# Gates with both activation halves as one 512-column matmul, and decay matrices loaded as broadcast rows through GpSimd's queue

## The chip, the cores and the metric

The kernel runs on one core of one Trainium2 chip. The metric is the device time of one execution in microseconds (us); the median of the runs stands for the kernel. The engines are named as in the profile: PE is TensorE's matmul side and PEld its weight loads, DVE is VectorE, ACT is ScalarE, POOL is GpSimd, SP is SyncE. A line such as L366 is a line of the kernel's file.

## The reference

Two layers of a hybrid model run over 256 tokens of width 2048 (batch 1), in float32. The first ("even") layer has a bidirectional gated delta rule, a differential attention and an attention over 256 memory tokens; the second ("odd") layer has a window attention, a latent attention and a memory attention. Each layer projects the normed input to all queries, keys, values and gates, multiplies every branch's output by a gated silu, and projects back.

```
h = rms_norm(x, norm_g) @ w_in
gq, gk, gv, gb, ga, gg, dq, dk, dv, dg, mq, mg = split_cols(h, EV_SPLITS)
y = concat([gdn_branch(...), diff_attention(...), memory_attention(...)])
return x + y @ w_out
```

The part that matters here is the decay of the delta rule, and the gate:

```
g = jnp.cumsum(g, axis=-1)                       # per chunk of 64, per head and direction
diff = g[..., :, None] - g[..., None, :]
decay = jnp.where(lower_incl, jnp.exp(jnp.where(lower_incl, diff, 0.0)), 0.0)
m = jnp.where(strict, jnp.einsum('bhncd,bhnsd->bhncs', k_beta, k) * decay, 0.0)
a_intra = jnp.where(lower_incl, jnp.einsum('bhncd,bhnsd->bhncs', q, k) * decay, 0.0)
o = o * jax.nn.silu(gate)                        # each branch
```

## The kernel before

**Matmuls in halves.** Every float32 weight and activation is split into a high half that the PE takes (fp32r) and a low rest. A product is then three matmuls: weights high by activations high, weights high by activations low, weights low by activations high. `load_split` brings a block of weights `w` (128 rows by 1024 columns, 512 KB) over SP's queue (L194), casts it to `wh` on ACT (L201) and subtracts `wl = w - wh` on DVE (L202). The activations lie channel-major in two tiles, `xH` and `xL` (16 tiles of 128 channels by 256 tokens).

**Three kinds of projection.** `gemm` (L218 to L220) has tokens on the output's partitions and streams up to 512 weight columns. `gemm_T` (L233 to L235) and `gate_T` (L365 to L367) are channel-major: 128 weight columns stay in the PE and the 256 tokens of `xH` or `xL` stream through. `gate_T` makes 256 gate channels from 16 channel tiles, two accumulators and three matmuls each, in twelve calls: 2 in the even layer (L965's loop), 10 in the odd one. Its two accumulators are scaled by `rsb` on DVE (L370), then come tanh on ACT (L371) and two multiplications on DVE (L372, L373). `gemm_out` (L254 to L256) is the output projection; it goes through the channel blocks of `y` in an order written out, for the even layer 8, 12, 16, 0, 4. Blocks 0 and 4 are the delta rule's output `o_gdn`, transposed on the PE by `gated_T` (L392) and split into halves by ACT (L154) and DVE (L155).

**The delta rule** works on two groups of four heads, two 128-token tiles `t` and two directions `d`. `gdn_rates` makes the cumulated decay `gcum` early (by 124 us). `keys_decay` makes for each group the keys `kT` (with `qk_tiles`, whose convolution on DVE and ACT writes the tiles `cc`, L697 to L704), and then for each `t` and `d` the decay matrix `E` (128 by 4x128): four PE transposes of a broadcast column of `gcum` (L757), four DVE instructions that subtract the column and add the mask (L759), and one exponential on ACT (L761). Later lines build `MnT` from it, invert triangles by substitution on DVE, and run the chunks: matmuls into `z` (L892) and `o` (L922), then add (L924), a sum of squares on ACT, a power on POOL (L145), scaling into `o_gdn` (L932) and the last gate multiplication (L352).

**What sets the order.** The Tile framework's scheduler orders each engine's instructions by its own simulated timeline, within the dependences of the tiles; `tc.issue_after(x)` holds an instruction until `x`. Each engine works through its row in order, and each DMA queue through its own. So a change in one place can move instructions far from it.

Of the kernel before, what the change touches and what calls it, by code (L numbers as in the profile page):

```python
# [87 lines left out]
def kernel(ctx: ExitStack, tc: tile.TileContext, a: dict, out: bass.AP):  # L88
# [46 lines left out]
    def bcm(ap, n):  # L135

        return ap.unsqueeze(1).to_broadcast([ap.shape[0], n, ap.shape[1]])

    def inv_sqrt(out_ap, ss, mul, eps, st="n"):

        shape = [ss.shape[0], ss.free_size()]
        t = spool.tile([P, 32], F32, tag="isq" + st, name="isq")
        tv = t[:shape[0], :shape[1]]
        V.tensor_scalar(tv, ss, mul, eps, op0=ALU.mult, op1=ALU.add)  # L144
        G.tensor_tensor(out_ap, tv, mhalf[:shape[0], :shape[1]], op=ALU.pow)  # L145

# [207 lines left out]

    def gate_T(wd, col, oT, H, L, rsb, pool, y=None):


        wv = wd.rearrange("(k p) c -> p k c", p=P)
        acc = [accp.tile([P, 512], F32, tag="acc", name="acc")[:, :S] for _ in range(2)]
        for k0 in range(0, NK, 4):  # L360
            wh, wl = load_split(wv[:, k0:k0 + 4, col:col + 256], 4, 256)
            for k in range(4):
                for i in range(2):
                    cs, kk = slice(i * P, (i + 1) * P), k0 + k
                    T.matmul(acc[i], lhsT=wh[:, k, cs], rhs=H[:, kk], start=kk == 0, stop=False)  # L365
                    T.matmul(acc[i], lhsT=wh[:, k, cs], rhs=L[:, kk], start=False, stop=False)  # L366
                    T.matmul(acc[i], lhsT=wl[:, k, cs], rhs=H[:, kk], start=False, stop=kk == NK - 1)  # L367
        g_, th = [pool.tile([P, 512], F32, tag="gt", name=n, bufs=4).rearrange("p (i s) -> p i s", i=2) for n in ("g_", "gth")]
        for i in range(2):
            V.tensor_tensor(g_[:, i], acc[i], rsb, op=ALU.mult)  # L370
        A.activation(th, g_, AF.Tanh, scale=0.5)  # L371
        V.scalar_tensor_tensor(th, th, 1.0, g_, op0=ALU.add, op1=ALU.mult)  # L372
        V.tensor_tensor(th if y else oT, th, oT, op=ALU.mult)  # L373
        if y:
            split(th, None, *y)
# [32 lines left out]

    xH = xpool.tile([P, NK, S], F32R, tag="xH", name="xH")
    xL = xpool.tile([P, NK, S], F32R, tag="xL", name="xL")  # L410

    bias_d = dpool.tile([2, 8, 512], F32, name="bias_d")
    NG = 480
    sg_d = dpool.tile([P, 2, NG], F32, name="sg_d")
# [106 lines left out]
    with tc.tile_pool(name="dif", bufs=2, reuse_waits="tile") as dp:  # L521
# [85 lines left out]
        def gdn_rates():  # L607
# [52 lines left out]
            V.tensor_tensor(be2, beta, e2, op=ALU.mult)  # L660
            return rsb, beta, nbeta, gl, gcum, e1, ne1, e2, be2

        qkv = diff_qkv(0)
        mem_split(0)
        rsb, beta, nbeta, gl, gcum, e1, ne1, e2, be2 = gdn_rates()
        diff_attention(0, *qkv)
# [57 lines left out]
    def cols_of(h0):  # L724
# [3 lines left out]
        return cols  # L728

    def keys_decay(h0):  # L730

        cols = cols_of(h0)


        kN = gp.tile([P, 2, 4, P], F32, tag="kN", name="kN", bufs=2)
        kT, ssk = qk_tiles(EV["gk"] + h0 * P, 8 + h0, "k", kN)
        rk, r2k, irk = [keep(8) for _ in range(3)]
        nb2, b2, be22 = [keep(16).rearrange("p (t d h) -> p t d h", t=2, d=2) for _ in range(3)]
        inv_sqrt(rk, ssk, 1.0, 4 * EPS)
        V.tensor_tensor(r2k, rk, rk, op=ALU.mult)  # L740
        V.scalar_tensor_tensor(irk, ssk, 4 * EPS, rk, op0=ALU.add, op1=ALU.mult)
        V.tensor_scalar(irk, irk, 0.5, None, op0=ALU.mult)
        r2b = r2k.rearrange("p (t h) -> p t h", t=2).unsqueeze(2).to_broadcast([P, 2, 2, 4])
        for dst, src in ((nb2, nbeta), (b2, beta), (be22, be2)):
            V.tensor_tensor(dst, src.rearrange("p (t d h) -> p t d h", t=2, d=2)[:, :, :, h0:h0 + 4], r2b, op=ALU.mult)

        E = gp.tile([P, 2, 2, 4, P], F32, tag="E", name="E", bufs=2)
        MnT = gp.tile([P, 2, 2, 4, P], F32, tag="MnT", name="MnT", bufs=2)
        for t in range(2):
            pg = ps_tile()  # L750
            for h in range(4):
                T.matmul(pg[:, h * P:(h + 1) * P], lhsT=kT[:, h, t * P:(t + 1) * P], rhs=kT[:, h, t * P:(t + 1) * P],
                         start=True, stop=True)
            for d in range(2):
                pb = ps_tile()
                for h in range(4):
                    T.transpose(pb[:, h * P:(h + 1) * P], cols(gcum, t, d)[:, h:h + 1].to_broadcast([P, P]), ident)  # L757
                for h in range(4):
                    V.scalar_tensor_tensor(E[:, d, t, h], pb[:, h * P:(h + 1) * P], cols(gcum, t, d)[:, h:h + 1],  # L759
                                           amask(d), op0=ALU.subtract, op1=ALU.add)  # L760
                A.activation(E[:, d, t], E[:, d, t], AF.Exp)  # L761
                for h in range(4):
                    V.scalar_tensor_tensor(MnT[:, d, t, h], pg[:, h * P:(h + 1) * P], nb2[:, t, d, h:h + 1],
                                           E[:, d, t, h], op0=ALU.mult, op1=ALU.mult)
        m_d = dpool.tile([16, 4, 32, 32], F32, tag="m_d", name="m_d", bufs=2)
        mv_ = MnT.rearrange("p d t h c -> p (d t h) c")
        for b in range(4):
            nc.sync.dma_start(m_d[:, b].rearrange("m i j -> i m j"), mv_[b * 32:(b + 1) * 32, :, b * 32:(b + 1) * 32])
        return kN, kT, E, MnT, irk, b2, be22, m_d.rearrange("m b i j -> (m b) i j")

# [13 lines left out]
    G.memset(vt, 0.0)  # L784
    G.memset(vt.rearrange("p i j -> p (i j)")[:, 0:1024:33], 1.0)
    tmp = gp.tile([P, 256], F32, name="tmp")
# [19 lines left out]
    for grp in range(2):  # L806
# [4 lines left out]
        Tm = gp.tile([P, 2, 2, 4, P], F32, tag="Tm", name="Tm")  # L811
        G.memset(Tm, 0.0)
        for dst, src in zip((Tm, Rm), tr_d[grp]):
# [129 lines left out]
    for g in range(2):  # L943
        hs = slice(2 * g, 2 * g + 2)
        gate_T(w0, EV["mg"] + 256 * g, o_mem[:, hs], xH, xL, rsb, opool2)
    for t in range(2):
# [9 lines left out]
    with tc.tile_pool(name="yp", bufs=2, reuse_waits="tile") as yp:  # L956
# [7 lines left out]
        def evac(g, t, ps):  # L964
            if not nxt:  # L965
                nxt.extend(xpool.tile([P, NK, S], F32R, tag=n, name=n + "1") for n in ("xH", "xL"))
            x_ = x1[:, t, 512 * g:512 * (g + 1)]
# [5 lines left out]
            if t == 1:  # L973
                split_T(lambda k, t: x1[:, t, k * P:(k + 1) * P], par[:, R_ODN:R_ODN + NK], range(4 * g, 4 * g + 4), *nxt)
        gemm_out(a["ev_w_out"][0], y, (8, 12, 16, 0, 4), evac,
                 [(4 * i, lambda i=i: gated_T(cols512(o_gdn, i), par[:, R_GDN:R_GDN + 1], y[4 * i])) for i in range(2)])
        opool_stack.close()
        xH, xL = nxt
        ss1 = spool.tile([P, 2], F32, tag="ssx", name="ss1")
# [13 lines left out]
    def gates(col, o_, k0, n):  # L993
        for g in range(0, n, 2):
            gate_T(w1, col + P * g, o_[:, g:g + 2], xH, xL, rsb1, yp, [x_[:, g % 4:g % 4 + 2] for x_ in y[k0 + g - g % 4]])

# [205 lines left out]
```

## Time and profile before

| what | value |
|---|---|
| median of 3 runs | 1206.33 us (1205.81 to 1206.83) |
| the profiled execution | 1208.67 us, span in the trace 1206.9 us |
| PE busy | 1190.3 us, 99% of the span |
| DVE, ACT, POOL busy | 839.8 (70%), 640.0 (53%), 109.8 us (9%) |
| granted clock of PE | 0.996 of full speed over the span |

The span is what the trace covers, from the first instruction to the last; the execution's own time is 1.8 us longer. The sums of the prediction are made on the profiled execution and then moved to the median, which lies 2.34 us lower. A busy PE is not a PE at its peak: a matmul counts as busy from its start to its modelled end, and consecutive ones overlap, so the distance from start to start says more than the mean of one.

### The profile page before, as it was taken

Reading aid. Unit: us, or ns where it says so; the run is one execution under the profiler, and the core shown is the slowest. Engines: PE = TensorE matmul, PEld = TensorE weight load, DVE = VectorE, ACT = ScalarE, POOL = GpSimd, SP = SyncE. Lnnn points to the kernel's source line nnn. Section 1 sums busy time; section 2 is a strip of 40 time slices with the busy share of each in tenths; the row PEclk is TensorE's granted clock in tenths of the full one; section 3 lists DMA queues with packets and bytes.
Section 4 is the critical chain, followed back from the end, with each engine's and each line's share of the span. In section 5 each row is a group of like instructions: output and inputs, shape, how many; then the busy total and the mean of one; then the engine's idle time right before and its main releaser. Section 6 shows DMA issues by size and latency. Waiting matters only on the chain.

```text
span 1206.9 us, 19842 instructions
## 1 busy us (share of the span) xinstructions
PE 1190.3 (99%) x7608; PEld 1063.2 (88%) x7608; DVE 839.8 (70%) x1450; ACT 640.0 (53%) x1117; POOL 109.8 (9%) x116
## 2 busy tenths in 40 slices
PE   9899999999999999999999999999999999999998
PEld 7678888788999999889988889999889899998887
DVE  5675876666889899857755555667766678876553
ACT  6664666455555454444654446566555555554432
POOL 0110112000101010002000001323310000000000
PEclk9899999999999999999999999999999999999999
DMA  9976675555655666653536656666556565555663
GB/s 333 350 225 230 215 236 162 175 165 167 174 152 137 168 176 192 194 142 82 187 105 209 206 167 185 179 184 194 160 158 203 164 208 158 159 157 166 201 210 121
DMA packets 183183, 221.95 MB, mean 184 GB/s; under 512 B 20536, under 2 KB 119608, under 8 KB 182576
## 3 DMA queue, kind: packets, MB, share of 16 engines
q1 hardware_dynamic: 172640, 201.09, 56.0%
q10 hardware_dynamic: 9552, 16.48, 3.9%
q0 software_dynamic: 896, 3.11, 0.8%
q8 instruction: 59, 0.97, 0.3%
q14 instruction: 36, 0.29, 0.1%
HBM read 214.36 MB, written 6.29 MB: 183 GB/s over the span
## 4 chain that ended last, share of the span: by engine, by line
PE 89%; DVE 4%; DMA 3%; ACT 2%; issue 1%; POOL 1%; SPq 0%; DVEq 0%; ACTq 0%; POOLq 0%
PE acc L219 14%; PE acc L220 13%; PE acc L218 13%; PE acc L254 6%; PE acc L256 6%; PE acc L255 6%; PE acc L366 4%; PE acc L367 4%; PE acc L365 4%; PE acc L235 3%; PE acc L233 3%; PE acc L234 3%; PE ps L165 3%; PE ps L892 1%; DVE wl L202 1%
## 5 line engine op out<-in xcount | busy, mean ns | idle before, releaser
L202 DVE TENSOR_TENSOR wl<-w,wh 128x1024 fp32r<-128x1024 f32 (+3 forms) x392 | 456.8, 1167 | 240.5 <-ACT wh L201 237.9
L201 ACT CAST wh<-w 128x1024 fp32r<-128x1024 f32 (+3 forms) x392 | 392.1, 1001 | 401.4 <-PE acc L220 141.3
L219 PE MATMUL acc<-wl,xH 128*128 128x512 f32 (+3 forms) x704 | 259.5, 370 | 3.0 <-DVE wl L202 3.0
L220 PE MATMUL acc<-wh,xL 128*128 128x512 f32 (+3 forms) x704 | 256.0, 365 | 0.0
L218 PE MATMUL acc<-wh,xH 128*128 128x512 f32 (+3 forms) x704 | 238.5, 366 | 2.7 <-ACT wh L201 2.7
L219 PEld LDWEIGHTS acc<-wl,xH 128*128 128x128 f32 x704 | 133.1, 189 | 24.2 <-DVE wl L202 5.4
L218 PEld LDWEIGHTS acc<-wh,xH 128*128 128x128 f32 x704 | 130.5, 189 | 21.1 <-ACT wh L201 4.2
L220 PEld LDWEIGHTS acc<-wh,xL 128*128 128x128 f32 x704 | 133.1, 189 | 17.1
L255 PE MATMUL acc<-wl,y 128*128 128x512 f32 x320 | 124.9, 391 | 0.0
L256 PE MATMUL acc<-wh,y 128*128 128x512 f32 x320 | 124.4, 390 | 0.0
L254 PE MATMUL acc<-wh,y 128*128 128x512 f32 x320 | 115.3, 392 | 1.3 <-ACT y L154 1.3
L235 PE MATMUL acc<-xH,wl 128*128 128x256 f32 x384 | 109.4, 286 | 1.1 <-DVE wl L202 1.1
L365 PE MATMUL acc<-xH,wh 128*128 128x256 f32 x384 | 110.1, 287 | 0.0
L366 PE MATMUL acc<-xL,wh 128*128 128x256 f32 x384 | 109.9, 286 | 0.0
L367 PE MATMUL acc<-xH,wl 128*128 128x256 f32 x384 | 109.6, 286 | 0.0
L233 PE MATMUL acc<-xH,wh 128*128 128x256 f32 x384 | 109.3, 285 | 0.0
L234 PE MATMUL acc<-xL,wh 128*128 128x256 f32 x384 | 109.1, 284 | 0.0
L145 POOL TENSOR_TENSOR r<-isq,kept 128x4 f32<-128x4 f32 (+2 forms) x27 | 49.7, 1841 | 400.4 <-DVE isq L144 384.1
L235 PEld LDWEIGHTS acc<-xH,wl 128*128 128x128 f32 x384 | 73.4, 191 | 1.7 <-DVE wl L202 1.7
L366 PEld LDWEIGHTS acc<-xL,wh 128*128 128x128 f32 x384 | 74.2, 193 | 0.3
L365 PEld LDWEIGHTS acc<-xH,wh 128*128 128x128 f32 x384 | 74.3, 194 | 0.2
L367 PEld LDWEIGHTS acc<-xH,wl 128*128 128x128 f32 x384 | 74.1, 193 | 0.0
(364 smaller groups left out, 1760.9 us busy)
## 6 DMA issues: line engine op xcount, KB each, us to landing
w<-in_ev_w_in_dram SPq DMA_DIRECT2D x136, 512.0 KB, 4.1
w<-in_od_w_in_dram SPq DMA_DIRECT2D x72, 512.0 KB, 3.9
w<-in_ev_w_out_dram SPq DMA_DIRECT2D x40, 512.0 KB, 3.7
w<-in_od_w_out_dram SPq DMA_DIRECT2D x40, 512.0 KB, 4.1
w<-in_od_w_in_dram SPq DMA_DIRECT2D x32, 384.0 KB, 3.4
w<-in_od_mem_w_kv_dram SPq DMA_DIRECT2D x16, 512.0 KB, 3.6
w<-in_ev_mem_w_kv_dram SPq DMA_DIRECT2D x16, 512.0 KB, 3.7
w<-in_od_w_in_dram SPq DMA_DIRECT2D x16, 288.0 KB, 2.9
```

The costliest lines, as they stand in the source:

```text
L201: A.copy(wh[:, :kn * n], w[:, :kn * n])
L202: V.tensor_tensor(wl[:, :kn * n], w[:, :kn * n], wh[:, :kn * n].bitcast(F32), op=ALU.subtract)
L218: T.matmul(o, lhsT=h, rhs=wh[:, k], start=first, stop=False)
L219: T.matmul(o, lhsT=h, rhs=wl[:, k], start=False, stop=False)
L220: T.matmul(o, lhsT=l, rhs=wh[:, k], start=False, stop=last)
L235: T.matmul(o, lhsT=wl[:, k], rhs=H[:, kk], start=False, stop=kk == NK - 1)
L254: T.matmul(acc[t], lhsT=h, rhs=wh[:, k], start=first, stop=False)
L255: T.matmul(acc[t], lhsT=h, rhs=wl[:, k], start=False, stop=False)
L256: T.matmul(acc[t], lhsT=l, rhs=wh[:, k], start=False, stop=last)
L365: T.matmul(acc[i], lhsT=wh[:, k, cs], rhs=H[:, kk], start=kk == 0, stop=False)
L366: T.matmul(acc[i], lhsT=wh[:, k, cs], rhs=L[:, kk], start=False, stop=False)
L367: T.matmul(acc[i], lhsT=wl[:, k, cs], rhs=H[:, kk], start=False, stop=kk == NK - 1)
```

## The change

`xH` and `xL` become the two halves of one tile `xHL` (channel tile, half, token), so that a channel tile's two halves lie side by side as 512 columns. `gate_T` streams them through the high weights in one matmul of 512 columns into a whole accumulator (now L369), and the low weights by the high activations into its first 256 columns (L370). Behind it ACT copies the second half out, DVE adds it to the first, and one DVE multiplication scales both channels.

For the decay matrices, `gdn_rates` transposes `gcum` once, writes the 32 rows to a scratch tensor in DRAM (`gc_d`), and makes `ngcum`, the negated column. `keys_decay` loads each `E[:, d, t]` (128 by 512, 256 KB) from four rows of `gc_d`, broadcast to all partitions: 8 DMAs on GpSimd's queue, held behind `held`, the last power (`inv_sqrt`) written before `keys_decay`. DVE then adds the mask in one instruction of 512 columns, and ACT takes four exponentials of 128 columns, each with its column of `ngcum` as bias. The PE transposes and the 32 DVE instructions go. A clearing of `Tm` on POOL is held behind that of the substitution's identity.

```diff
     def inv_sqrt(out_ap, ss, mul, eps, st="n"):
...
-        G.tensor_tensor(out_ap, tv, mhalf[:shape[0], :shape[1]], op=ALU.pow)
+        pows.append(G.tensor_tensor(out_ap, tv, mhalf[:shape[0], :shape[1]], op=ALU.pow))
+        return pows[-1]
...
-    def gate_T(wd, col, oT, H, L, rsb, pool, y=None):
+    def gate_T(wd, col, oT, HL, rsb, pool, y=None):
...
-        acc = [accp.tile([P, 512], F32, tag="acc", name="acc")[:, :S] for _ in range(2)]
+        acc = [accp.tile([P, 512], F32, tag="acc", name="acc") for _ in range(2)]
...
-                    T.matmul(acc[i], lhsT=wh[:, k, cs], rhs=H[:, kk], start=kk == 0, stop=False)
-                    T.matmul(acc[i], lhsT=wh[:, k, cs], rhs=L[:, kk], start=False, stop=False)
-                    T.matmul(acc[i], lhsT=wl[:, k, cs], rhs=H[:, kk], start=False, stop=kk == NK - 1)
+                    T.matmul(acc[i], lhsT=wh[:, k, cs], rhs=HL[:, kk].rearrange("p h s -> p (h s)"), start=kk == 0, stop=False)
+                    T.matmul(acc[i][:, :S], lhsT=wl[:, k, cs], rhs=HL[:, kk, 0], start=False, stop=kk == NK - 1)
...
-            V.tensor_tensor(g_[:, i], acc[i], rsb, op=ALU.mult)
+            A.copy(g_[:, i], acc[i][:, S:])
+            V.tensor_tensor(g_[:, i], acc[i][:, :S], g_[:, i], op=ALU.add)
+        V.tensor_tensor(g_, g_, bcm(rsb, 2), op=ALU.mult)
...
+            ngcum = sm("ngcum")
+            V.tensor_scalar(ngcum, gcum, -1.0, None, op0=ALU.mult)
+            pt = ps_tile()
+            T.transpose(pt[:32, :P], gcum, ident)
+            gr = dp.tile([32, P], F32, name="gr", bufs=1)
+            V.tensor_copy(gr, pt[:32, :P])
+            G.dma_start(gc_d, gr)
...
+    held = pows[-1].ins
...
+        E = gp.tile([P, 2, 2, 4, P], F32, tag="E", name="E", bufs=2)
+        for t in range(2):
+            for d in range(2):
+                r_ = gc_d[t * 16 + d * 8 + h0:t * 16 + d * 8 + h0 + 4]
+                with tc.issue_after(held):
+                    G.dma_start(E[:, d, t].rearrange("p h c -> p (h c)"), bass.AP(r_.tensor, r_.offset, [[0, P], [1, 4 * P]]))
...
-                pb = ps_tile()
+                V.tensor_tensor(E[:, d, t], E[:, d, t], bcm(amask(d), 4), op=ALU.add)
                 for h in range(4):
-                    T.transpose(pb[:, h * P:(h + 1) * P], cols(gcum, t, d)[:, h:h + 1].to_broadcast([P, P]), ident)
-                for h in range(4):
-                    V.scalar_tensor_tensor(E[:, d, t, h], pb[:, h * P:(h + 1) * P], cols(gcum, t, d)[:, h:h + 1],
-                                           amask(d), op0=ALU.subtract, op1=ALU.add)
-                A.activation(E[:, d, t], E[:, d, t], AF.Exp)
+                    A.activation(E[:, d, t, h], E[:, d, t, h], AF.Exp, bias=cols(ngcum, t, d)[:, h:h + 1])
...
-    G.memset(vt.rearrange("p i j -> p (i j)")[:, 0:1024:33], 1.0)
+    eye = G.memset(vt.rearrange("p i j -> p (i j)")[:, 0:1024:33], 1.0)
...
-        G.memset(Tm, 0.0)
+        with tc.issue_after(eye.ins):
+            G.memset(Tm, 0.0)
```

The scheduler then orders the rows anew. On GpSimd's row the eight loads of `E` stand in one block directly behind the held power `r<-isq` (128 by 8), and ahead of the powers of the keys (`kept<-isq`). The changed kernel's row there:

```order
L147 TENSOR_TENSOR r<-isq,kept 128x4 x2
L147 TENSOR_TENSOR r<-isq,kept 128x8
L761 DMA E<-gc_d 128x512 x8
L147 TENSOR_TENSOR kept<-isq,kept 128x8 x2
L805 MEMSET Rm 128x1024
```

In the kernel before, the same power was followed by the keys' powers at once:

```order
L145 TENSOR_TENSOR r<-isq,kept 128x4 x2
L145 TENSOR_TENSOR r<-isq,kept 128x8
L145 TENSOR_TENSOR kept<-isq,kept 128x8 x2
L784 MEMSET Rm 128x1024
```

On DVE's row the eight additions of the mask (L780), for both groups, stand among the convolution of the next keys and the subtractions `wl` (now L205), a little behind the scaling of the memory queries (`nat`). The changed kernel's row from that scaling on:

```order
L280 TENSOR_TENSOR nat<-acc,r 128x512 x2
L715 TENSOR_TENSOR kept<-acc,kept 128x256
L205 TENSOR_TENSOR wl<-w,wh 128x1024
L780 TENSOR_TENSOR E<-E,kept 128x512
L719 SCALAR_TENSOR_TENSOR cc<-kept,cc 128x256
L780 TENSOR_TENSOR E<-E,kept 128x512
...
L780 TENSOR_TENSOR E<-E,kept 128x512 x2
L293 TENSOR_REDUCE nm<-ps 128x2
L780 TENSOR_TENSOR E<-E,kept 128x512 x2
L205 TENSOR_TENSOR wl<-w,wh 128x1024
L722 SCALAR_TENSOR_TENSOR kT<-kT,cc 128x256
```

Between the two `wl` shown stand a third one and all eight additions. Before, the same place held no work for `E`; the 32 DVE instructions of L759 stood after the keys' convolution, and the `kT` of the last row stood ahead of the last `wl` shown.

On PE's row the end of the delta rule (group 1's last matmuls `ps<-Tm,E`, before L922, now L944) moves behind nearly the whole output projection of the blocks 8, 12 and 16. Before:

```order
L922 MATMUL ps<-Tm,E 128x128
L255 MATMUL acc<-wl,y_6514 128x512
...
L254 MATMUL acc<-wh,y_6514 128x512
L922 MATMUL ps<-Tm,E 128x128 x15
L255 MATMUL acc<-wl,y_6514 128x512
...
L254 MATMUL acc<-wh,y_6515 128x512 x2
L392 MATMUL acc<-kept,o_gdn 128x128 x4
L255 MATMUL acc<-wl,y_6515 128x512
```

Here 28 matmuls of the projection stand between the last L922 and the first transposes of `o_gdn` (L392). In the changed kernel:

```order
L259 MATMUL acc<-wh,y_6431 128x512
L397 MATMUL acc<-kept,o_gdn 128x128 x2
L944 MATMUL ps<-Tm,E 128x128
L397 MATMUL acc<-kept,o_gdn 128x128 x4
L944 MATMUL ps<-Tm,E 128x128 x15
L397 MATMUL acc<-kept,o_gdn 128x128
L257 MATMUL acc<-wh,y_6427 128x512
L258 MATMUL acc<-wl,y_6427 128x512
...
L259 MATMUL acc<-wh,y_6427 128x512
L397 MATMUL acc<-kept,o_gdn 128x128 x5
```

The lone transpose (L397) behind the fifteen L944 takes the columns 384 to 511 of `o_gdn`, of the first token tile. The last 32 of them are gated by the same multiplication (columns 480 to 751, now L355) that needs group 1's output; and the first matmul of block 0 behind it (L257) needs that transpose, split into halves. Only 12 matmuls of the projection then stand between it and the next transposes.

## Rows read from the trace of the kernel before

**Rows 1.** The page: busy time of each engine; GB/s in 40 slices.
```profile
PE 1190.3 (99%) x7608; PEld 1063.2 (88%) x7608; DVE 839.8 (70%) x1450; ACT 640.0 (53%) x1117; POOL 109.8 (9%) x116
...
GB/s 333 350 225 230 215 236 162 175 165 167 174 152 137 168 176 192 194 142 82 187 105 209 206 167 185 179 184 194 160 158 203 164 208 158 159 157 166 201 210 121
```

**Rows 2.** Waits of TensorE, whole span: us in total, times, longest.
```profile
PE acc L254 <- ACT y L154: 1.3, 1, 1.3
PE acc L235 <- DVE wl L202: 1.1, 2, 0.7
PE ps L892 <- ACT MnT L905: 1.0, 1, 1.0
```

**Rows 3.** Timeline of PE, a gate_T, then the output projection: start, us, line.
```profile
1089.38 0.28 PE L367 MATMUL acc<-xH,wl 128*128 128x256 f32 x1
...
1090.82 0.28 PE L367 MATMUL acc<-xH,wl 128*128 128x256 f32 x1
...
1093.26 0.40 PE L256 MATMUL acc<-wh,y 128*128 128x512 f32 x1
...
1094.42 0.39 PE L255 MATMUL acc<-wl,y 128*128 128x512 f32 x1
...
1100.09 0.39 PE L256 MATMUL acc<-wh,y 128*128 128x512 f32 x1
```

**Rows 4.** Groups by line, the decay matrices: busy us, mean ns.
```profile
L759 DVE SCALAR_TENSOR_TENSOR E<-ps,kept 128x128 f32<-128x128 f32 x32 | 9.0, 353 | 0.3 <-PE ps L757 0.3
```

**Rows 5.** Timeline of PE, the first four decay transposes and the row behind.
```profile
368.25 0.60 PE L757 MATMUL ps<-kept 128*128 128x128 f32 x4
368.60 0.36 PE L234 MATMUL acc<-xL,wh 128*128 128x256 f32 x1
```

**Rows 6.** Stretches: busy PE, PEld, DVE, ACT, POOL; clock, DMA share, GB/s.
```profile
320.00:330.00 10.00, 10.00 (x86) 10.00 (x85) 9.29 (x20) 6.08 (x11) 0.00 (x0) 1.00 0.60 164
...
368.00:395.00 27.00, 27.00 (x234) 27.00 (x233) 26.55 (x81) 14.80 (x23) 4.41 (x2) 1.00 0.51 132
```

**Rows 7.** Timeline of POOL, DVE and PE, 309 to 327 us.
```profile
309.21 2.62 POOL L145 TENSOR_TENSOR r<-isq,kept 128x8 f32<-128x8 f32 x1 [4.19 <-DVE isq L144]
...
313.11 1.28 DVE L277 TENSOR_TENSOR nat<-acc,r 128x512 f32<-128x512 f32 x2
...
314.31 0.42 DVE L697 TENSOR_TENSOR kept<-acc,kept 128x256 f32<-128x256 f32 x1
...
321.52 1.22 DVE L202 TENSOR_TENSOR wl<-w,wh 128x1024 fp32r<-128x1024 f32 x1
...
326.36 0.28 PE L235 MATMUL acc<-xH,wl 128*128 128x256 f32 x1
```

**Rows 8.** DMA issues of GpSimd's queue: KB each, median us to landing.
```profile
mk_d<-kT POOLq DMA_DIRECT2D x2, 512.0 KB, 4.8
mv_d<-mvN POOLq DMA_DIRECT2D x2, 512.0 KB, 3.8
...
sg<-sg_d POOLq DMA_DIRECT2D x2, 240.0 KB, 5.4
```

**Rows 9.** Timeline of POOL, the two issues of mv_d.
```profile
159.51 0.53 POOL L604 DMA_DIRECT2D mv_d<-mvN  x1 [9.60 <-ACT mvN L154]
160.37 0.53 POOL L604 DMA_DIRECT2D mv_d<-mvN  x1 [0.34 <-DVE mvN L155]
```

**Rows 10.** Timeline of DVE and PE, end of the delta-rule block, group 1.
```profile
612.96 0.69 DVE L924 TENSOR_TENSOR MnT<-ps,MnT 128x512 f32<-128x512 f32 x1 [3.90 <-PE ps L922]
...
616.22 1.23 DVE L202 TENSOR_TENSOR wl<-w,wh 128x1024 fp32r<-128x1024 f32 x1 [0.58 <-ACT wh L201]
...
618.34 0.80 DVE L352 TENSOR_TENSOR o_gdn<-th,o_gdn 128x272 f32<-128x272 f32 x2
...
623.62 0.60 PE L392 MATMUL acc<-kept,o_gdn 128*128 128x128 f32 x4
...
625.50 0.50 PE L254 MATMUL acc<-wh,y 128*128 128x512 f32 x1 [1.29 <-ACT y L154]
```

More of the change, by code (lines that the diff above doesn't have):

```diff
@@ L137, in bcm @@
         return ap.unsqueeze(1).to_broadcast([ap.shape[0], n, ap.shape[1]])
+    pows = []
     def inv_sqrt(out_ap, ss, mul, eps, st="n"):
@@ L407, with both_halves @@
     opool_stack = ExitStack()
-    xH = xpool.tile([P, NK, S], F32R, tag="xH", name="xH")
-    xL = xpool.tile([P, NK, S], F32R, tag="xL", name="xL")
+    def both_halves(name):
+        x_ = xpool.tile([P, NK, 2, S], F32R, tag="xHL", name=name)
+        return x_, x_[:, :, 0], x_[:, :, 1]
+    xHL, xH, xL = both_halves("xHL0")
     bias_d = dpool.tile([2, 8, 512], F32, name="bias_d")
+    gc_d = dpool.tile([32, P], F32, name="gc_d")
     NG = 480
@@ L660, in gdn_rates @@
             V.tensor_tensor(be2, beta, e2, op=ALU.mult)
-            return rsb, beta, nbeta, gl, gcum, e1, ne1, e2, be2
+            ngcum = sm("ngcum")
[5 more added lines that the diff above has]
+            G.dma_start(gc_d, gr)
+            return rsb, beta, nbeta, ngcum, e1, ne1, be2
         qkv = diff_qkv(0)
         mem_split(0)
-        rsb, beta, nbeta, gl, gcum, e1, ne1, e2, be2 = gdn_rates()
+        rsb, beta, nbeta, ngcum, e1, ne1, be2 = gdn_rates()
         diff_attention(0, *qkv)
@@ L745, in keys_decay @@
             V.tensor_tensor(dst, src.rearrange("p (t d h) -> p t d h", t=2, d=2)[:, :, :, h0:h0 + 4], r2b, op=ALU.mult)
-        E = gp.tile([P, 2, 2, 4, P], F32, tag="E", name="E", bufs=2)
         MnT = gp.tile([P, 2, 2, 4, P], F32, tag="MnT", name="MnT", bufs=2)
@@ L944 @@
         hs = slice(2 * g, 2 * g + 2)
-        gate_T(w0, EV["mg"] + 256 * g, o_mem[:, hs], xH, xL, rsb, opool2)
+        gate_T(w0, EV["mg"] + 256 * g, o_mem[:, hs], xHL, rsb, opool2)
     for t in range(2):
@@ L965, in evac @@
             if not nxt:
-                nxt.extend(xpool.tile([P, NK, S], F32R, tag=n, name=n + "1") for n in ("xH", "xL"))
+                nxt.extend(both_halves("xHL1"))
             x_ = x1[:, t, 512 * g:512 * (g + 1)]
@@ L973, in evac @@
             if t == 1:
-                split_T(lambda k, t: x1[:, t, k * P:(k + 1) * P], par[:, R_ODN:R_ODN + NK], range(4 * g, 4 * g + 4), *nxt)
+                split_T(lambda k, t: x1[:, t, k * P:(k + 1) * P], par[:, R_ODN:R_ODN + NK], range(4 * g, 4 * g + 4), *nxt[1:])
         gemm_out(a["ev_w_out"][0], y, (8, 12, 16, 0, 4), evac,
@@ L977 @@
         opool_stack.close()
-        xH, xL = nxt
+        xHL, xH, xL = nxt
         ss1 = spool.tile([P, 2], F32, tag="ssx", name="ss1")
@@ L994, in gates @@
         for g in range(0, n, 2):
-            gate_T(w1, col + P * g, o_[:, g:g + 2], xH, xL, rsb1, yp, [x_[:, g % 4:g % 4 + 2] for x_ in y[k0 + g - g % 4]])
+            gate_T(w1, col + P * g, o_[:, g:g + 2], xHL, rsb1, yp, [x_[:, g % 4:g % 4 + 2] for x_ in y[k0 + g - g % 4]])
     with tc.tile_pool(name="at1", bufs=2, reuse_waits="tile") as dp:
```

## The prediction

> **What bounds the kernel now.** I read the page first: PE is busy for 99% of the span, DVE for 70%, ACT for 53%, GpSimd for 9% [rows 1]. So time goes down in two ways only: fewer or shorter matmuls on PE, or fewer waits of PE. The waits come next: those that the change touches are 1.3 us for the halves of `y`, 1.1 us in two waits of `gemm_T` (L235) for `wl`, and 1.0 us inside the delta rule [rows 2]. Then I read the PE's timeline for what a matmul costs, which is the distance from one start to the next and not the mean in the groups: between 256-column matmuls it is 0.120 us (12 steps from 1089.38 to 1090.82), between 512-column ones 0.227 us (25 steps from 1094.42 to 1100.09), but 0.232 in the first five behind 256-column ones (1093.26 to 1094.42) [rows 3]. Last come the two places where instructions move: the stretch from 309 to 327 us [rows 7] and the end of the delta rule at 612 to 626 us [rows 10].
>
> **gate_T: -5.0 us.** 12 calls x 16 channel tiles x 2 accumulators are 384 groups. Three matmuls of 256 columns cost 0.36 us; one of 512 and one of 256 cost 0.347 us [rows 3]. The difference, 13 ns, times 384 is 5.0 us. It says that a matmul costs some 13 ns beyond what its columns cost, once each. Since the new matmuls change between 512 and 256 columns, the step of 0.232 could hold throughout; then it is 8 ns and 3.1 us, the other bound. I take 5.0, as the longer run shows the steady step. The evacuation grows by two ACT copies and a DVE addition per call, all behind the accumulators and ahead of a tanh whose reader comes later; DVE has 30% idle, so I cost it at nothing. If that cover were gone, each of the twelve calls could cost about one 512-column addition, 0.6 us [rows 7].
>
> [...]
>
> **Decay transposes: -2.7 us.** Four transposes (L757) hold PE for 0.35 us (368.25 to 368.60) [rows 5]; 32 of them, one for each instruction of L759 [rows 4], are eight such fours, 2.8 us. One new transpose of `gcum` gives back 0.1.
>
> **DVE after 368 us: -1.1 us.** DVE is busy 26.55 of 27 us at 368 to 395 [rows 6], of which 9.0 us are the 32 instructions of L759 [rows 4]. The two waits of L235 for `wl` (1.1 us) [rows 2] come shortly behind. With that work gone DVE catches up. Bounds: 0 (what is late there is something else) and -1.1; I take the whole.
>
> **E's masks at 315 us: +2.0 us.** The additions don't vanish, they move into a stretch in which DVE is busy 9.29 of 10 us [rows 6]. Each is a 512-column float32 addition like `nat`, of which two take 1.20 us (313.11 to 314.31) [rows 7], so eight take 4.8 us. Between `kept` and the third `wl` behind it DVE's row is as before, with the eight additions put in and one `kT` of 256 columns, half such an addition, put behind: 4.5 us more. That `wl`, at 321.52 before, starts at about 326.0 and ends at 327.2; its first reader on PE started at 326.36 [rows 7]. So PE waits 0.9 us if every E has landed when DVE asks for it, and later waits don't add much, since a PE that has waited comes later to the next block.
> Has it landed? The held power ends at 311.83 [rows 7]. The eight issues take GpSimd about 0.53 us each [rows 9]. GpSimd's transfers landed 3.8 us (`mv_d`) to 5.4 us (`sg`) after the issue [rows 8]. The first addition is due at about 315.8, so the first E lands just in time by the one and is 1.4 us late by the other; the eighth is due at 325.4. All eight are 2.1 MB; beside 164 GB/s for the weights [rows 6], and with 350 GB/s as the most that a slice of the span shows [rows 1], they need 11 us, which ends near 324. So the lower bound is 0.9 us, and with the first E late by 1.4 it is 2.3. I take 2.0, since E, like `sg`, is a load from DRAM by this queue. The upper bound: 2 MB at the rate of `mk_d`, 512 KB in 4.8 us [rows 8], are 19.2 us, E ends at 331.0, 5.6 us late, and the cost is 6.5 us. The 32 small exponentials stand on ACT behind the masks; ACT is 61% busy there [rows 6].
>
> **The end of the delta rule: +4.1 us.** Before, from the addition of `o` (612.96) to the last gate multiplication (618.34 + 0.80) a chain of 6.2 us runs over DVE, ACT, DVE, POOL and DVE; a `wl` (616.22 to 617.45) stands in it [rows 10], without which it is about 5.6 us. 28 projection matmuls of 0.23 us covered it. What remained was one wait of 1.3 us for the split of `y` behind the transposes (623.62 to 625.50) [rows 10]. Now there stands between the first half of L944 and the transpose that needs this chain only the second half, eight matmuls, about 0.9 us. PE would wait 4.7 us for the chain, again 1.3 for the split, and about 0.4 for the second token tile, whose chain ends some 1.7 us behind the first and which 12 matmuls cover: 6.4 us. Of before, 1.3 and 1.0 us (L254 and L892) [rows 2] go, as they are the same passage. Net 4.1. Bounds: 0, if DVE and PE arrive there with other distances than the row suggests, and 5.4, if the 1.0 stays and the split takes longer.
>
> **The sum.** -5.0 - 2.7 - 1.1 + 2.0 + 4.1 = -2.7 us on the profiled 1208.67, which gives 1205.97; the median lies 2.34 us below the profiled execution, so **1203.6 us**. A change under 0.2% (2.4 us) can hardly be told from none, so this forecast stands just on the faster side.
>
> **The rivals.**
> *All gain, no loss.* DVE's slack and E's early landing hide the masks (+0.9 or less), and the end of the delta rule is covered. For it: DVE has 30% idle in the whole. Against it: the row of PE leaves 0.9 us of cover for a chain of 5.6. Sum -8.8 to -7.9: 1197.5 to 1198.4.
> *E lands late (slower).* Every E waits in GpSimd's queue behind the held power; DVE's addition stands ahead of `wl`, and all further `wl` are queued behind it, so each us by which the eighth E passes 325.4 is a us of PE. Without E's term the sum is -4.7, so slower than 1208.7 it ends from a cost of 7.1 on, that is, if the eighth E lands after 331.6, against 331.0 in my upper bound. One after another at 5.4 us they would end at 355, which costs some 30 us: 1231. Against that: the two `mv_d` were issued 0.86 us apart [rows 9] with 3.8 us to landing [rows 8], so they were under way together.
> [...]
> *The merged matmul brings little.* If its step in `gate_T` is nearer to that of two of 256 columns (0.237 against 0.227), for instance because each change of length costs something, as the step of 0.232 hints [rows 3], the saving is about 1 us instead of 5.0 and the time 1207.6, no change.
>
> **Chances.** The forecast's own case (E slightly late, the wait at the end there): 0.50, with 1200.5 to 1206.5. All gain: 0.20, 1196.5 to 1200.5. Little from the merged matmul, or both losses at their upper bounds: 0.20, 1206.5 to 1209. E late: 0.10, above 1208.7. The first case has three fifths of its weight under 1203.9, which with the second makes 0.50 faster; slower is 0.11 (E late, and a little of the third), the rest, 0.39, no change. The range that leaves out two in ten is 1197.5 to 1208.5.
>
> **What would show it.** gate_T right: start to start 0.227 and 0.120 us in L369 and L370, and PE's busy time some 8 us less. E right: a wait of L238 (before L235) or L223 for `wl` of 1 to 3 us near 326 us, and POOL issues from 311.8 on; E late: DVE waiting for the DMA at L780. The end: a wait of L397 for the gate's DVE multiplication of 4 to 5 us, then L257 for ACT. DVE's share at 368 to 395 falls from 98% to about 70%. I would be wrong above all if the scheduler's row at the end does not cost what its distances say, or if PE comes there later because it waited before.

## The result and the profile after

The changed kernel takes 1213.88 us (median of 6 runs, 1210.58 to 1216.37) against 1206.24 us of the kernel before: ratio 1.0065, 95% interval 1.005 to 1.0081. It is slower by 0.65%, where 1203.6 us and a little faster were forecast. The profiled execution took 1212.39 us, with a span of 1210.6 us, 3.7 us more than before. The page's busy times, to be read beside [rows 1]:

```profile
PE 1185.5 (98%) x7193; PEld 1039.9 (86%) x7193; DVE 844.7 (70%) x1440; ACT 650.8 (54%) x1165; POOL 111.2 (9%) x125
```

PE does less than before, as it should, and yet the span is longer: the time went into waits. These are the waits of PE that answer to [rows 2], and one that has no counterpart there (us in total, times, longest):

```profile
PE acc L397 <- DVE o_gdn L355: 4.1, 1, 4.1
PE ps L886 <- issue: 3.7, 1, 3.7
PE acc L238 <- DVE wl L205: 2.9, 2, 1.6
...
PE acc L257 <- ACT y L157: 1.5, 2, 0.8
...
PE acc L236 <- ACT wh L204: 0.8, 1, 0.8
```

The first and the fourth are the end of the delta rule, foreseen. The second was foreseen nowhere: "issue" means that PE waited for nothing the profile shows. PE's timeline there:

```profile
519.25 0.44 PE L886 MATMUL ps<-Rm,X 32*32 32x32 f32 x3 [1.24 <-DMA Rm<-r_d]
...
520.34 0.87 PE L886 MATMUL ps<-Rm,X 32*32 32x32 f32 x57
524.90 0.21 PE L886 MATMUL ps<-Rm,X 32*32 32x32 f32 x1 [3.69 <-issue]
525.04 0.79 PE L369 MATMUL acc<-xHL,wh 128*128 128x512 f32 x1
525.63 0.41 PE L370 MATMUL acc<-xHL,wl 128*128 128x256 f32 x1
525.84 0.63 PE L369 MATMUL acc<-xHL,wh 128*128 128x512 f32 x1
```

PE stops ahead of the last of 64 equal records, with no wait for data in the profile, and afterwards a pair L369, L370 takes 0.64 us (525.63 to 526.27 by the next pair), not 0.35. The stretches show why (columns as in [rows 6]; the clock is the figure behind the five engines):

```profile
520.00:524.00 4.00, 1.21 (x117) 1.10 (x108) 0.41 (x1) 1.45 (x4) 0.00 (x0) 0.59 0.93 314
524.00:528.00 4.00, 3.10 (x10) 2.58 (x10) 1.27 (x3) 0.00 (x0) 0.00 (x0) 0.50 0.03 9
...
624.00:628.00 4.00, 0.17 (x1) 0.17 (x1) 2.68 (x9) 2.00 (x14) 2.01 (x2) 0.82 0.38 129
628.00:632.00 4.00, 3.22 (x8) 2.28 (x9) 2.40 (x6) 0.69 (x1) 0.00 (x0) 0.50 0.00 0
```

Behind each of the two long waits the granted clock is 0.50 for some microseconds in which PE has work, against 1.00 ahead of them (512 to 520 and 616 to 624 us). So such a passage costs more than its wait. At the second wait the clock fell while PE stood idle (0.50 from 626.5 to 633.3 us). At the first it fell at 520.7 us, half a microsecond before the wait, behind the small matmuls, and stayed low to 530.9. The kernel before also lost some clock behind the same small matmuls, without such a wait (0.50 from 524.0 to 527.4 us):

```profile
524.00:528.00 4.00, 4.00 (x40) 3.77 (x41) 1.31 (x4) 1.52 (x3) 0.00 (x0) 0.57 0.56 186
```

So there the wait is not the only cause of the low clock; what the changed kernel adds is that it lasts 10.2 us and not 3.4. The spread of the runs goes with the clock: the six runs of the changed kernel go from 1210.58 us at a mean clock of 0.993 to 1216.37 us at 0.988.

The end of the delta rule, to be read beside [rows 10]:

```profile
620.24 3.51 PE L944 MATMUL ps<-Tm,E 128*128 128x128 f32 x30
627.83 0.48 PE L397 MATMUL acc<-kept,o_gdn 128*128 128x128 f32 x1 [4.08 <-DVE o_gdn L355]
629.09 0.80 PE L257 MATMUL acc<-wh,y 128*128 128x512 f32 x1 [0.78 <-ACT y L157]
...
633.92 0.71 PE L397 MATMUL acc<-kept,o_gdn 128*128 128x128 f32 x5
635.35 0.50 PE L257 MATMUL acc<-wh,y 128*128 128x512 f32 x1 [0.72 <-ACT y L157]
```

And the masks of E, on DVE, to be read beside [rows 7]; the last line is the `wl` that stood at 321.52 before:

```profile
315.64 0.69 DVE L780 TENSOR_TENSOR E<-E,kept 128x512 f32<-128x512 f32 x1 [1.17 <-DMA E<-gc_d]
...
324.23 1.28 DVE L780 TENSOR_TENSOR E<-E,kept 128x512 f32<-128x512 f32 x2
325.43 1.21 DVE L205 TENSOR_TENSOR wl<-w,wh 128x1024 fp32r<-128x1024 f32 x1
```

The first E came 1.17 us late, the others in time. PE waits 1.57 us for this `wl`:

```profile
326.70 0.39 PE L238 MATMUL acc<-xHL,wl 128*128 128x256 f32 x1 [1.57 <-DVE wl L205]
```

### The profile page after: what moved, and what is told of

It is laid out like the page before. It is cut to its first block, busy times and chain, and to the rows that moved or that the text cites. A ratio compares the mean times of both kernels' runs of the same rounds, so it can differ in the third digit from the quotient of the medians.

```text
span 1210.6 us, 19091 instructions
## 1 busy us (share of the span) xinstructions
PE 1185.5 (98%) x7193; PEld 1039.9 (86%) x7193; DVE 844.7 (70%) x1440; ACT 650.8 (54%) x1165; POOL 111.2 (9%) x125
## 3 DMA queue, kind: packets, MB, share of 16 engines
q1 hardware_dynamic: 172640, 201.09, 56.3%
## 4 chain that ended last, share of the span: by engine, by line
PE 90%; DVE 3%; DMA 3%; issue 1%; ACT 1%; POOL 1%; SPq 0%; DVEq 0%; ACTq 0%; POOLq 0%
PE acc L222 14%; PE acc L223 14%; PE acc L221 14%; PE acc L369 7%; PE acc L257 6%; PE acc L258 6%; PE acc L259 6%; PE acc L370 4%; PE acc L238 3%; PE acc L237 3%; PE acc L236 3%; PE ps L168 3%; PE ps L914 1%; DVE wl L205 1%; DMA xnat<-in_memN_dram 1%
## 5 line engine op out<-in xcount | busy, mean ns | idle before, releaser
L205 DVE TENSOR_TENSOR wl<-w,wh 128x1024 fp32r<-128x1024 f32 (+3 forms) x392 | 456.8, 1168 | 235.4 <-ACT wh L204 229.3
L222 PE MATMUL acc<-wl,xHL 128*128 128x512 f32 (+3 forms) x704 | 258.5, 368 | 2.3 <-DVE wl L205 2.3
L223 PE MATMUL acc<-wh,xHL 128*128 128x512 f32 (+3 forms) x704 | 256.1, 365 | 0.0
L221 PE MATMUL acc<-wh,xHL 128*128 128x512 f32 (+3 forms) x704 | 238.1, 366 | 2.8 <-ACT wh L204 2.8
L222 PEld LDWEIGHTS acc<-wl,xHL 128*128 128x128 f32 x704 | 132.7, 188 | 22.4 <-DVE wl L205 4.0
L221 PEld LDWEIGHTS acc<-wh,xHL 128*128 128x128 f32 x704 | 130.2, 188 | 21.1 <-ACT wh L204 4.2
L223 PEld LDWEIGHTS acc<-wh,xHL 128*128 128x128 f32 x704 | 132.8, 189 | 16.9
L369 PE MATMUL acc<-xHL,wh 128*128 128x512 f32 x384 | 138.4, 404 | 0.0
L257 PE MATMUL acc<-wh,y 128*128 128x512 f32 x320 | 116.6, 395 | 1.5 <-ACT y L157 1.5
L238 PE MATMUL acc<-xHL,wl 128*128 128x256 f32 x384 | 108.9, 285 | 2.9 <-DVE wl L205 2.9
L236 PE MATMUL acc<-xHL,wh 128*128 128x256 f32 x384 | 109.4, 285 | 0.8 <-ACT wh L204 0.8
L237 PE MATMUL acc<-xHL,wh 128*128 128x256 f32 x384 | 108.9, 284 | 0.0
L370 PE MATMUL acc<-xHL,wl 128*128 128x256 f32 x384 | 107.8, 285 | 0.0
L369 PEld LDWEIGHTS acc<-xHL,wh 128*128 128x128 f32 x384 | 73.0, 191 | 20.1 <-issue 3.9
L238 PEld LDWEIGHTS acc<-xHL,wl 128*128 128x128 f32 x384 | 73.4, 192 | 3.3 <-DVE wl L205 3.3
L236 PEld LDWEIGHTS acc<-xHL,wh 128*128 128x128 f32 x384 | 73.6, 192 | 1.0 <-ACT wh L204 1.0
L370 PEld LDWEIGHTS acc<-xHL,wl 128*128 128x128 f32 x384 | 73.7, 192 | 0.9
L237 PEld LDWEIGHTS acc<-xHL,wh 128*128 128x128 f32 x384 | 73.6, 192 | 0.0
```

Source lines behind the costliest of these rows:

```text
L205: V.tensor_tensor(wl[:, :kn * n], w[:, :kn * n], wh[:, :kn * n].bitcast(F32), op=ALU.subtract)
L221: T.matmul(o, lhsT=h, rhs=wh[:, k], start=first, stop=False)
L222: T.matmul(o, lhsT=h, rhs=wl[:, k], start=False, stop=False)
L223: T.matmul(o, lhsT=l, rhs=wh[:, k], start=False, stop=last)
L236: T.matmul(o, lhsT=wh[:, k], rhs=H[:, kk], start=kk == 0, stop=False)
L237: T.matmul(o, lhsT=wh[:, k], rhs=L[:, kk], start=False, stop=False)
```

## The experiments

Every ratio is against the kernel before, run on the same chip in turn, with its 95% interval.

**One part alone.** `e1_gate_only` is the kernel before with gate_T's edit, `e2_decay_only` the changed kernel without it (here the lines of e2 against the changed kernel):

```diff
-                    T.matmul(acc[i], lhsT=wh[:, k, cs], rhs=HL[:, kk].rearrange("p h s -> p (h s)"), start=kk == 0, stop=False)
+                    T.matmul(acc[i], lhsT=wh[:, k, cs], rhs=H[:, kk], start=kk == 0, stop=False)
+                    T.matmul(acc[i], lhsT=wh[:, k, cs], rhs=L[:, kk], start=False, stop=False)
```

> The kernel before with the change of gate_T alone (one tile for both halves, 512 columns, new evacuation); the decay matrices as before. Theory: the end of the delta rule moves because the scheduler's plan of the shorter gate_T moves it, not because of the decay matrices; its row has 16 matmuls ps<-Tm,E directly ahead of the lone transpose here too. Then PE waits there 4 to 5 us for the gate's multiplication, and the clock falls behind the wait; with 2.9 us saved in gate_T (384 times 7.5 ns) the ratio is 1.002 to 1.005. Rival: the late end belongs to the decay matrices; then no wait over 1.5 us there and a ratio of 0.997 to 0.999.

Measured: 1.0007 (0.9995 to 1.002). Its waits:

```profile
PE acc L394 <- DVE o_gdn L352: 3.7, 1, 3.7
```

So in these plans the late end of the delta rule comes with gate_T and not with the decay matrices: here too 12 projection matmuls follow the lone transpose, where e2 below has 29 of them ahead of the first transpose. The time is under the expected range. Its steps in gate_T are those of the changed kernel (0.233 and 0.117 us), so that 3.8 us are saved and not the 2.9 that the expectation counted, and its list of waits has none for "issue".

> The changed kernel with gate_T's three matmuls of 256 columns and its old evacuation put back; the decay matrices come from broadcast rows. Theory: 2.7 us of PE are saved, 1.7 us lost at 325 us for wl behind the masks, nothing at the end of the delta rule, whose last ps<-Tm,E stand 29 projection matmuls ahead of the first transpose: ratio 0.998 to 1.000. Rival: loads through GpSimd's queue disturb more than DVE (weights late, waits of L221 to L238 beyond 3 us in all): ratio over 1.002.

Measured: 1.0018 (1.0002 to 1.0033), above the expected range. The end is as before (one wait of 1.3 us for `y`), and the masks cost what they cost in the changed kernel:

```profile
PE acc L238 <- DVE wl L205: 2.6, 2, 1.3
```

The decay edit by itself is thus no gain in the place where it was put. The rival's sign came true, but its mechanism is not seen: the waits of L221 to L238 are 7.6 us in all, against 6.8 in the same lines of the kernel before, and those of L221 are 2.2, less than the 2.7 there. What makes the run slower than the sum of its waits is not shown; its ten runs have a median clock of 0.995, against 0.998 of the kernel before on the same chip.

**The wait for "issue".** `e3_phase` makes PE's instruction stream longer ahead of everything:

```diff
-        for _ in range(WARM):
+        for _ in range(WARM - 6):
             T.matmul(pt[:, :P], lhsT=ones, rhs=ones, start=True, stop=True)
+        for _ in range(38):
+            T.matmul(pt[:, :1], lhsT=ones, rhs=ones[:, :1], start=True, stop=True)
```

> The changed kernel with 38 matmuls of one column and 6 of 128 in place of the 12 warm-up matmuls at the start, so that PE's instruction stream is 128 instructions longer ahead of everything else (half of one 16 KB fetch at 64 bytes each). Theory: the wait of 3.7 us inside the last 32 by 32 matmuls (L886 or one line off) is one for instructions: a 16 KB fetch that was due at about 514 us started at 522.37 us, and its place in the stream decides; with the stream moved by half a fetch the wait there goes or falls under 1 us, or it turns up at another place of that stretch. The time is 2 to 5 us less than the changed kernel's 1213.9 us. Rival: the wait is for data (the Rm blocks or DVE's copy of X) and stays at 3 to 4 us in the same matmuls.

Measured: 1.0049 (1.0032 to 1.0065). The wait is gone (the waits list no "issue"; what is left there is 2.0 us for Rm). The time fell by 1.9 us only, since the longer warm-up delayed the start: the one-column matmuls hold PE for 16.2 us, the first projection matmul starts at 19.79 us instead of 6.66, and GpSimd's issue of `sg_d` stands at 116.01 us, against 107.82 in the changed kernel. Behind that point it is 7.4 us shorter (spans 1211.4 and 1210.6). That the start would pay was not in my expectation, and some rows moved in the plan, so e3 alone is weak evidence.

`e5_shift36` goes the other way and leaves every row where it was:

```diff
-        for _ in range(WARM):
-            T.matmul(pt[:, :P], lhsT=ones, rhs=ones, start=True, stop=True)
+        for _ in range(3):
+            T.matmul(pt[:, :512].rearrange("p (a b) -> p a b", b=128), lhsT=ones, rhs=ones.unsqueeze(1).to_broadcast([P, 4, 128]), start=True, stop=True)
```

> The changed kernel with 3 warm-up matmuls of 512 columns in place of the 12 of 128: every row of every engine behind them is the same, but PE's instruction stream is 36 instructions shorter ahead of it (9 matmuls of 4). Theory: the place where PE runs out of fetched instructions is fixed in the stream; it was 4 instructions ahead of the end of the 32 by 32 matmuls and now lies 32 behind that end, some 8 pairs L369 and L370 of 0.35 us later. The wait is then at about 1 us instead of 3.7, ahead of an L369 or L370, or gone; the time is 3 to 5 us under the changed kernel's 1213.9. Rival: the wait belongs to the matmuls' data or to the end of that block; it stays at the last L886 with 3 us or more.

Measured: 1.0006 (0.9992 to 1.002). With the same rows on all engines and nothing changed but the warm-up matmuls, no wait for "issue" is left. The ratio is 0.0036 to 0.0059 under the two that the changed kernel has (1.0042 and 1.0065), 4 to 7 us, where 3 to 5 were expected; they were not run side by side.

`e9_shift_back` (8 warm-up matmuls of 128 columns and 8 of one; the 12 of the changed kernel stand in its trace as 24 matmuls and 24 weight loads, four records each, so these are 16 instructions more):

> The changed kernel with 8 warm-up matmuls of 128 columns and 8 of one column in place of the 12: the same rows on every engine, and a PE stream 16 instructions longer ahead of everything (4 matmuls of 4). Theory: the place where PE runs dry moves 16 instructions (8 matmul records) the other way, so the wait of 3 to 5 us stands inside the last 32 by 32 matmuls, with about 9 records of L886 behind it in place of 1. Rival: the wait stays ahead of the last record, or is gone.

Measured, in a single run: 1210.07 us. The wait did not move by 8 records, it was gone: the instructions came earlier here (below). `e12_wide_rows` takes away the small pieces of Rm:

```diff
-                nc.sync.dma_start(dv_[b * 32:(b + 1) * 32, :, b * 32:(b + 1) * 32], src[:, b].rearrange("m i j -> i m j"))
+                if dst is Rm:
+                    nc.sync.dma_start(dst[b * 32:(b + 1) * 32].rearrange("p d t h c -> p (d t h c)")[:, 512 * b:512 * b + 512],
+                                      src.rearrange("m b i j -> (m b i j)").rearrange("(b i n) -> b i n", b=4, i=32)[b])
+                else:
...
```

> The changed kernel with the loads of Rm taking rows of 512 numbers (2 KB) in place of 16 pieces of 32 (128 bytes), into other columns of Rm: the same bytes, issues and rows on PE but for one swap, a sixteenth of the pieces. It leaves the inverted triangles of Rm in the wrong places, so the delta rule's numbers are wrong. Theory: PE's instruction fetch near 514 us is late because the DMA engines are full of the small pieces of Rm; without them the fetch starts by about 518 us, the wait of PE inside the 32 by 32 matmuls goes, the time is 4 to 8 us under the changed kernel's. Rival: the weights' bursts alone hold the fetch back; it still starts after 521 us and the wait stays at 3 us or more.

> The changed kernel itself once more, beside the run with wide rows on the same chip. Theory: the wait ahead of the last 32 by 32 matmul record stands in this execution too, at 3 to 4 us, with a fetch that starts 8 us after it is due; ratio 1.004 to 1.008. Rival: it is a chance event of the first profile, and is missing or elsewhere here, while the ratio is the same.

Measured on one chip: 1.0042 (1.0023 to 1.006) for the changed kernel again, 1.0004 (0.9993 to 1.0016) with wide rows. In the second profile of the changed kernel the wait stands ahead of the same record:

```profile
524.96 0.21 PE L886 MATMUL ps<-Rm,X 32*32 32x32 f32 x1 [3.88 <-issue]
```

With wide rows it is gone; so is the wait for Rm (1.2 and 0.4 us in the two profiles of the changed kernel), which is part of the gain. The DMA queues of the first changed run, from 500.5 to 522.3 us (queue, kind, packets, MB, share):

```profile
q1 hardware_dynamic: 7942, 4.89, 80.0%
q14 instruction: 1, 0.01, 0.1%
```

and of the run with wide rows, from 501.6 to 518 us:

```profile
q1 hardware_dynamic: 5255, 4.12, 90.4%
q8 instruction: 1, 0.02, 0.5%
q14 instruction: 1, 0.01, 0.1%
```

Queue q8, of the kind `instruction`, goes with PE's stream: over the whole run it moves 56 packets of 16384 bytes, 0.92 MB, which is 64 bytes for each of PE's 7193 matmuls and 7193 weight loads, a packet for some 257 of them. With the 7608 matmuls of the kernel before it moves 59 packets, with the 7257 of e3 57. So I take it for the queue that brings PE's instructions. In the changed kernel none comes between 500.5 and 522.3 us, while PE goes through a burst of 64 small matmuls and one of 128; it starts at 522.37, has landed at 523.48, and PE goes on at 524.90. With wide rows it starts at 516.14.

The traces also say where PE stops. In all three profiles that have the long wait (the changed kernel, e13 and e4) PE had started 3158 matmuls and 3159 weight loads, 6317 records, when it stopped, although the packet started at three different times (522.37, 522.53 and 525.38). So the place is fixed in the stream, as the theory of e5 said. In e5 the packet was as late (521.97), but record 6317 lay behind the burst: PE had used 6301 when the packet started and 6307 when it had landed, and did not stop. In e9 the packet started at 518.62, with 6071 used. Whether PE stopped in these runs thus hung on two things: what it still had to run at that place of the stream, and when the packet came.

What makes the packet late is not isolated. The wide rows take away 3840 of q1's 172640 packets, but the DMA engines are no less busy in the stretch (90.4% against 80.0%), and e9 has its packet at 518.62 with all the pieces in place.

**The end of the delta rule.** `e4_gate_cut` cuts the gate's multiplication where the groups meet, so that no transpose of block 0 needs group 1 (`cut` is 512 - 480 = 32):

```diff
-            V.tensor_tensor(o_get(t), th, o_get(t), op=ALU.mult)
+            o_ = o_get(t)
+            for c in ([slice(0, cut), slice(cut, n)] if cut else [slice(0, n)]):
+                V.tensor_tensor(o_[:, c], th[:, c], o_[:, c], op=ALU.mult)
```

> The changed kernel with the gate multiplication of columns 480 to 751 cut into two, 480 to 511 and 512 to 751, so that no transpose of block 0 needs group 1. 24 projection matmuls then stand between the last ps<-Tm,E and the transposes that need it. Theory: the wait of 4.1 us goes, the one for the split of y stays (about 1.3 us), the clock does not fall there; 5 to 7 us less than the changed kernel's 1213.9 us, so a ratio of 1.000 to 1.002. Rival: the chain of group 1 is late by more than its cover, and the wait comes back in front of block 4's transposes: ratio over 1.004.

Measured: 1.0017 (0.9996 to 1.0037), from runs that spread widely (1202.68 us at a clock of 0.997 to 1212.08 at 0.990); the wait of 4.1 us became one of 1.0 (L399, the transposes' line here), the wait for "issue" stays at 4.1 us. The clock still falls at that end, to 0.50 for 3.4 us (from 636.5).

> The gate multiplication cut at column 512 and the 36 instructions less, both, on the changed kernel. Theory: the two big losses are independent, so both waits go; what is left are 6.5 us saved on PE (3.8 in gate_T, 2.7 in the decay transposes) against 2 us for wl behind the masks and 1 us more at 416 us: ratio 0.996 to 0.999. Rival: a third loss takes their place, or the clock: ratio over 1.001.

Measured: 0.996 (0.9945 to 0.9975), on the chip and beside the runs of e5. Both waits are gone and the losses add: e6 against e5 puts the end at 0.0046, 5.5 us (with both intervals some 3 to 8).

> The kernel before with the change of gate_T and with the gate multiplication cut at column 512; the decay matrices as before. Theory: 3.8 us saved in gate_T, no wait of over 1.5 us at the end of the delta rule, no wait for wl at 325 us: ratio 0.996 to 0.999. Rival: the saving of gate_T is given back elsewhere: ratio over 0.9995.

Measured: 0.996 (0.9945 to 0.9975). Against e1, run on another chip, the cut is again worth 0.0047. And e7, without the new decay matrices, comes out as e6 does with them.

**Where the masks stand.** `e8_load_by_act` issues the loads from ACT (`A.dma_start` for `G.dma_start`), which also lets the scheduler put them earlier; `e11_early_only` keeps GpSimd's queue and changes one number, `e10_early_cut_shift` does so on top of e6:

```diff
-    held = pows[-1].ins
+    held = pows[-5].ins
```

> The changed kernel with the eight loads of E issued by ACT's queue instead of GpSimd's; the scheduler then puts loads, masks and exponentials far earlier (before the 16th weight block of the memory keys is through), and the end of the delta rule stands with 28 projection matmuls of cover again. Theory: the losses at 325 us and at the end both come from where the plan put the rows, so both go: waits of L238 at most 1.5 us, of L397 none; ratio 0.995 to 0.999. Rival: the masks cost PE as much wherever DVE takes them, or ACT's issues make wh late (waits of L221 over 4 us): ratio over 1.000.

Measured: 0.9983 (0.9968 to 0.9997). The end and the waits of L238 are gone, but the masks, put in among the memory keys, make `wl` late there instead: waits of L222 of 6.2 us in all, against 2.3 in the changed kernel.

> The changed kernel with three edits: the gate multiplication cut at column 512, the 36 instructions less in the warm-up, and the loads of E held behind the fifth last power (about 213 us) instead of the last (312 us), so that the masks fall where DVE is busy 13.6 of 25 us (225 to 250 us of the run with cut and shift). Theory: no wait for wl behind the masks and none of over 0.5 us at 412 to 425 us; about 3 us less than the run with cut and shift alone: ratio 0.993 to 0.996. Rival: the masks and loads cost PE as much there: ratio 0.996 to 0.999.

Measured: 0.9942 (0.9928 to 0.9956), as expected.

> The changed kernel with the one edit that the loads of E are held behind the fifth last power. The plan then has 28 projection matmuls of cover at the end of the delta rule. Theory: no wait of over 1.5 us there and none for wl at 325 us; whether PE runs dry near 520 us hangs on the stream alone, which is as long as before the edit up to there, so that wait may stay. Ratio 0.994 to 0.997 without it, 0.998 to 1.003 with it. Rival: the loads through GpSimd's queue cost by themselves, wherever they are: ratio over 1.003.

Measured: 0.9928 (0.9911 to 0.9945), 1198.62 us, faster than both kernels and than expected. Its waits on the lines in question:

```profile
PE acc L257 <- ACT y L157: 1.3, 1, 1.3
...
PE acc L238 <- DVE wl L205: 0.2, 1, 0.2
PE ps L894 <- issue: 0.2, 1, 0.2
```

The loads stand at 211.62 us on GpSimd's row, and the masks from 217.08 to 225.45 us, ahead of the stretch that the expectation of e10 named. DVE is busy for 8.89 of 9 us there (217 to 226) and waited 2.75 us for the first E, and yet PE waits only 0.5 us for `wl` between 205 and 255 us. So a busy DVE alone does not make a place bad. The queue and the bytes are the same as in the changed kernel, but the one index also gave another plan, with 28 matmuls of cover at the end and no long wait for "issue", so the 14 to 16 us between the two are not those of the masks alone.

## Why the prediction was wrong

The kernel came out 10.3 us above the forecast. The step that failed most is one that the sum put at nothing: PE's instructions, for which PE waited 3.7 us inside ready work, 4.6 to 7 us with what followed. Next come three terms of the sum: DVE after 368 us, whose sign was wrong (2.1 us), the end of the delta rule, which left out the lower clock (1.4 us), and gate_T, sized too large (1.2 us).

**gate_T (-5.0): the right mechanism, too large.** In the changed kernel the steps are 0.233 us from L369 to L370 and 0.117 back (medians over some 360 pairs), 0.350 in all: 10 ns saved and not 13, 3.8 us. I had taken the steady step of 512 columns over the 0.232 that follows a change of length [rows 3]; here every matmul follows one. The step of 0.237 that the third rival supposed no run shows.

**Decay transposes (-2.7): not shown.** No run measured them alone. e6 and e7 have the same ratio; with 2.5 us for the masks in e6 and 1.1 us at 416 us, against 0.6 in e7, that leaves room for them. e2, where the decay edit stands by itself, does not show them: it is 2.2 us slower, where -2.7 with the waits near 325 and 416 us would give about nothing.

**DVE after 368 us (-1.1): wrong.** DVE did get freer (23.88 of 27 us, before 26.55 [rows 6]), but the waits near 416 us grew from 1.1 to 2.1 us (0.8 for `wh`, 1.3 for `wl`). DVE's load from 368 to 395 us does not set them. In the kernel before, the longer of the two waits (0.75 us at 413.15) is for a `wl` that stood behind a copy for which DVE had been idle for 3.5 us, until a transfer landed. So the load ahead of it had been worked off:

```profile
410.45 1.12 DVE L783 COPY Rm<-Rm 64x1024 f32<-64x1024 f32 x1 [3.49 <-DMA Rm<-m_d]
...
411.89 1.21 DVE L202 TENSOR_TENSOR wl<-w,wh 128x1024 fp32r<-128x1024 f32 x1
```

In the changed kernel DVE stands idle at the same copy, but the `wl` for which PE waits is a later one, and the plan has put four additions of 512 columns (L850) and two reductions ahead of it:

```profile
410.00 1.11 DVE L804 COPY Rm<-Rm 64x1024 f32<-64x1024 f32 x1 [2.97 <-DMA Rm<-m_d]
...
414.07 1.88 DVE L850 TENSOR_TENSOR E<-ps,E 128x512 f32<-128x512 f32 x3
...
417.84 1.22 DVE L205 TENSOR_TENSOR wl<-w,wh 128x1024 fp32r<-128x1024 f32 x1
```

A share of 98% in the stretch ahead led me past it. In e11, which has its decay matrices earlier, L236 and L238 wait 0.2 us each.

**E's masks (+2.0): right**, place and size (1.6 us, with the first E 1.17 us late and the last in time). The slower rival, E late through GpSimd's queue, did not happen; the eight loads, 2.1 MB, were through by 322.7 us, 5.2 to 9.0 us after their issues, beside a DVE that was busy for 9.84 of the 11 us from 312 to 323.

**The end of the delta rule (+4.1): right in mechanism, undersized.** Waits of 4.1, 0.8 and 0.7 us stand where they were forecast. Less the 2.3 us of before they are 3.3, under the term; but from 626.5 to 633.3 us PE had a clock of 0.50, and the passage cost 5.5 us (e6 against e5).

**Left out: PE's instructions.** This step is missing in the sum. It cost 4.6 us (e13 against e12 on one chip) to 7 us (e5 and e6 against the runs without the shift, not run side by side); up to 1.2 of the 4.6 us can be the wait for Rm. Nothing in the profile before showed such a wait, and the order of the rows shows none. The DMA records did hold a hint: before, too, no q8 packet came from 496.1 to 517.4 us. It did no harm there, since it came ahead of the burst of 128 small matmuls (521.85).

Put together with what was measured, and with the -2.7 that no run shows: -3.8 - 2.7 + 1.0 + 1.6 + 5.5 + 4.6 = +6.2 us, where the two comparisons of the changed kernel gave 1.0042 and 1.0065, 5.1 and 7.8 us. The profiled execution before also lay 2.3 us over its median and the one after 1.5 us under its own, so that the two traces differ by less than the medians do.

**Open:** why the packet of instructions is late. It came earlier in the one profile without the 128-byte pieces (e12), and earlier too with 16 warm-up instructions more (e9). In what order the DMA engines serve the queues no run showed.

## What to carry to other kernels

An edit that shortens one stage lets an automatic planner move others: read the new row around every place where little work covers a chain, and price the cover there first. A load that is held until some point is best tried at several such points; here one index turned a loss into a gain (1.0042 to 1.0065 became 0.9928). And where a burst of small matmuls meets a burst of DMA, count PE's instructions: here a wait of 3.7 us with no releaser, which went when the warm-up alone got longer or shorter, was one for instructions.

## What the runs showed of the hardware

Two things that I had not expected. First, PE ran dry in the middle of ready work: 127 of 128 small matmuls started within 1.7 us (519.25 to 520.98), and the next 16 KB packet of instructions, which at 64 bytes each is 256, started 23 us after the one before it (499.08 to 522.37), while PE had used up 546 instructions. Second, a passage with a wait of 4 us had the granted clock at 0.50 for 10.2 us (from 520.7) and for 6.8 us (from 626.5), with PE at work again for 5 to 6 us of each; there 512-column matmuls started 0.43 us apart instead of 0.227.
